# One-level Strassen passes of a GEGLU MLP: C11 kept in PSUM, staging loads issued by ScalarE, sums without negated forms

**Chip, cores, metric.** One core of one Trainium2 chip. The metric is the device time of the whole program in microseconds (us). This program runs on one core, so a single run has no state of its own; every run counted here was classed as fast.

## The reference

```python
x      (8, 1024, 1024) float32        w_gate, w_up (1024, 4096)      w_down (4096, 1024)

gate = x @ w_gate
up   = x @ w_up
gate = 0.5 * gate * (1 + np.tanh(np.sqrt(2 / np.pi) * (gate + 0.044715 * gate ** 3)))
h    = gate * up
return (h @ w_down).astype(np.float32)
```

## The kernel before

The 8192 tokens are worked off in eight passes of 1024, all in float16 with float32 sums. Passes 0 to 2 multiply gate and up with one level of a Strassen-like scheme (seven half-size products P1 to P7 in place of eight). Passes 3 to 7 use two levels with sums of weights that passes 1 and 2 have prepared and stored to HBM. After each pass comes a down product. Pass 0 loads the weights as float32 into small staging tiles and lets ScalarE cast them; passes 1 and 2 load and cast them with GpSimd. In pass 0 the kernel also forms and stores sums of w_down.

One "pair" of a one-level pass makes 256 columns of h. Its 14 slots are the products for gate (w=0) and up (w=1), each of four 512-column matmuls:

```python
SEQ = [
    ("P1", 0), ("P1", 1), ("P5", 0), ("P6", 0), ("P6", 1), ("P5", 1), ("P7", 0),
    ("P7", 1), ("P2", 0), ("P4", 0), ("P4", 1), ("P2", 1), ("P3", 0), ("P3", 1),
]
AFTER1 = {                       # work behind the product of that slot
    1: ["snap s1 0"],            # ScalarE: copy P1 out of bank "a" to SBUF ...
    2: ["snap s1 1"],
    4: ["snap s2 0"],            # ... before P6 accumulates onto the same bank
    5: ["snap s2 1"],
    7: ["snap s3 0"],
    8: ["snap s3 1", "add s3 0"],
    9: ["gelu s3", "add s3 1", "add s1 0"],
    10: ["gelu21", "prod s3", "gelu s1"],
    11: ["h21"],
    12: ["add s1 1"],
    13: ["prod s1", "add s2 0"],
    14: ["add s2 1"],
}                                # gelu s2 and prod s2 follow in the next pair
CHAIN = {"P1": "a", "P6": "a", "P7": "a", "P4": "a", "P5": "b", "P3": "b", "P2": "c"}
```

"add" is VectorE (PSUM bank plus snapshot), "gelu" ScalarE, "prod" a GpSimd product gelu(gate) x up of two SBUF tiles, "h21" a VectorE product straight from PSUM. The rest that the argument touches:

```python
def load_stage(u):               # pass 0: 512 KB of float32 weights
    ...
        nc.sync.dma_start(out=staging(u), in_=w_v[w][:, k, q * 512 : (q + 1) * 512])

def wd_store(q):                 # pass 0: seven stores of w_down sums
    ...
        nc.sync.dma_start(out=dst(v), in_=src)

def load_raw(p, q):              # passes 1 and 2: 512 columns of both weights, cast by the DMA
    ...
            nc.gpsimd.dma_start(out=raw(p, q)[:, w], in_=w_v[w][:, :, q * 512 : (q + 1) * 512])

# gate_up_one(p), pair i, q, e = divmod(i, 2)
if p == 0:
    ...
            if s // 14 == e:
                k = s % 14 + 1
                at(k, cast_stage, 8 * (q + 1) + u)       # ScalarE
                at(k, load_stage, 8 * (q + 1) + u + 4)   # into the tile just cast
    ...
elif e == 0:
    at(1, load_raw, p, q + 1)
...
if i == (12 if p == 0 else 4) and p + 1 < NPASS:
    at(2, cast_x, p + 1)         # GpSimd: the next pass's x to float16, HBM to HBM
```

## Time and profile before

| | |
|---|---|
| time, three runs | 2392.85 us median (2390.52 to 2394.59) |
| all 54 runs of this kernel in this study | 2390.2 us median and mean |
| pass 0, one-level gate and up | 252.6 us in the profile |
| passes 1 and 2, the same | 220.4 and 218.8 us |
| each two-level pass, each down product | 181.65 and 96.69 us, no gap |

In all views PE is TensorE's matmuls, PEld its weight loads, DVE VectorE, ACT ScalarE, POOL GpSimd and SP SyncE; a q behind a name is the engine's sequencer, L464 a line of the kernel, and square brackets hold the idle time before an instruction and what ended it. The page of the profiled execution gives the totals of each engine and the costliest groups (busy us, mean ns of one, idle time just before and its main releaser):

```profile
PE 2298.2 (96%) x14656; PEld 1435.1 (60%) x14656; DVE 1484.2 (62%) x2103; ACT 962.1 (40%) x1850; POOL 693.4 (29%) x821
...
L486 POOL TENSOR_TENSOR h_a<-tmp 128x512 f16<-128x512 f32 x144 | 204.9, 1424 | 447.2 <-DVE tmp L479 392.8
...
L475 ACT COPY tmp<-ps 128x512 f32<-128x512 f32 x288 | 163.7, 583 | 77.5 <-PE ps L464 74.2
```

PE is busy nearly all the time, so only its gaps in passes 0 to 2 can be won. The two groups are those that the change touches: 144 GpSimd products, a third of which (those of s1) go away, and 288 ScalarE copies, a third of which get another destination. The views of waits, chain and windows stand in the prediction.

### The profile page before, as it was taken

What the parts mean: (1) busy time and instruction counts of PE and PEld (TensorE: products, weight loads), DVE (VectorE), ACT (ScalarE), POOL (GpSimd) and SP (SyncE); (2) the same over time, 40 slices, a digit from 0 to 9 for tenths busy, and PEclk for the clock granted to TensorE, in tenths of its full rate; (3) what the DMA queues carried; (4) which work ended last, traced back from release to release, by engine and by line L of the source; (5) the groups of instructions that cost most, each with busy time, mean ns of one, the idle gap of its engine ahead of it and who ended that gap; (6) DMA issues with size and microseconds to landing.
All of it is one profiled execution on the core that took longest, in us unless ns stands there. A gap on an engine that the chain in (4) does not pass through costs nothing.

```text
span 2392.6 us, 38449 instructions
## 1 busy us (share of the span) xinstructions
PE 2298.2 (96%) x14656; PEld 1435.1 (60%) x14656; DVE 1484.2 (62%) x2103; ACT 962.1 (40%) x1850; POOL 693.4 (29%) x821
## 2 busy tenths in 40 slices
PE   6977999899999899999999999999999999999999
PEld 3433444344444344688747886488846887478854
DVE  5855627888358885467735677266754667356760
ACT  5755205454034551255403552155512554045520
POOL 1432203332023330045402542044401443024520
PEclk9988999999999999999999999999999999999999
DMA  8989757978679887798858988599867988578862
GB/s 277 281 228 251 233 153 191 214 182 236 213 172 226 190 222 248 248 307 288 269 196 268 314 279 258 195 274 324 274 219 245 310 282 273 196 269 277 281 212 106
DMA packets 259944, 579.23 MB, mean 242 GB/s; under 512 B 76016, under 2 KB 119024, under 8 KB 244976
## 3 DMA queue, kind: packets, MB, share of 16 engines
q1 hardware_dynamic: 221312, 520.16, 64.6%
q0 software_dynamic: 38448, 56.63, 14.0%
q8 instruction: 114, 1.87, 0.3%
q14 instruction: 70, 0.57, 0.1%
HBM read 520.09 MB, written 113.25 MB: 265 GB/s over the span
## 4 chain that ended last, share of the span: by engine, by line
PE 64%; DMA 5%; DVE 1%; issue 1%; POOL 0%; ACT 0%; SPq 0%; POOLq 0%; DVEq 0%; ACTq 0%
PE ps L665 38%; PE ps L760 24%; DMA ring<-in_w_up_dram 4%; PE ps L464 2%; DVE ring L294 1%; DVE tmp L479 0%; DMA w_ops<-x_sums 0%; POOL ring L279 0%; DVE x_sums L198 0%; POOL h_a L486 0%; ACT tmp L475 0%; DVE h_s L198 0%; DVE h_a L494 0%; ACT tmp L716 0%; SPq L383 0%
## 5 line engine op out<-in xcount | busy, mean ns | idle before, releaser
L665 PEld LDWEIGHTS <-ring 128*128 128x128 f16 x8320 | 812.9, 98 | 96.4
L642 POOL TENSOR_TENSOR h_a<-tmp 128x256 f16<-128x256 f32 x600 | 438.4, 746 | 954.3 <-ACT tmp L630 898.4
L760 PE MATMUL ps<-ring,h_a 128*128 128x512 f16 x3072 | 665.7, 379 | 0.0
L665 PE MATMUL ps<-x_sums,ring 128*128 128x256 f16 x5760 | 654.9, 273 | 0.0
L464 PEld LDWEIGHTS <-ring 128*128 128x128 f16 x2688 | 267.1, 99 | 422.7 <-issue 114.8
L760 PEld LDWEIGHTS <-h_a 128*128 128x128 f16 x3072 | 300.2, 98 | 361.8
L464 PE MATMUL ps<-x_sums,ring 128*128 128x512 f16 x1536 | 371.8, 393 | 76.2 <-ACT tmp L475 68.4
L627 DVE TENSOR_TENSOR tmp<-tmp,ps 128x512 f32<-128x512 f32 x600 | 387.1, 684 | 89.5 <-ACT tmp L612 63.4
L612 ACT COPY tmp<-ps 128x512 f32<-128x512 f32 x480 | 280.2, 585 | 272.4 <-PE ps L665 106.4
L716 ACT ACTIVATE tmp<-ps 128x512 f32<-128x512 f32 x128 | 76.4, 597 | 690.2 <-PE ps L760 690.2
L625 DVE TENSOR_TENSOR tmp<-ps,tmp 128x512 f32<-128x512 f32 x320 | 213.6, 688 | 214.9 <-PE ps L665 131.0
L486 POOL TENSOR_TENSOR h_a<-tmp 128x512 f16<-128x512 f32 x144 | 204.9, 1424 | 447.2 <-DVE tmp L479 392.8
L665 PE MATMUL ps<-x_b,ring 128*128 128x256 f16 x2560 | 305.6, 273 | 0.0
L630 ACT ACTIVATE tmp<-tmp 128x256 f32<-128x256 f32 x600 | 241.3, 416 | 136.4 <-DVE tmp L627 89.5
L720 DVE SCALAR_TENSOR_TENSOR tmp<-ps,tmp 128x512 f32<-128x512 f32 x96 | 66.4, 692 | 350.8 <-ACT tmp L716 218.0
L464 PE MATMUL ps<-x_b,ring 128*128 128x512 f16 x1152 | 269.4, 384 | 4.3 <-ACT ring L272 2.3
L479 DVE TENSOR_TENSOR tmp<-ps,tmp 128x512 f32<-128x512 f32 x288 | 190.1, 681 | 126.4 <-ACT tmp L475 118.6
L475 ACT COPY tmp<-ps 128x512 f32<-128x512 f32 x288 | 163.7, 583 | 77.5 <-PE ps L464 74.2
L294 DVE TENSOR_TENSOR ring<-ring 128x1024 f16<-128x1024 f16 x192 | 159.6, 845 | 22.1 <-DMA ring<-in_w_up_dram 17.9
L484 ACT ACTIVATE tmp<-tmp 128x512 f32<-128x512 f32 x144 | 90.9, 631 | 188.8 <-DVE tmp L479 188.8
L760 PE MATMUL ps<-ring,h_s 128*128 128x512 f16 x512 | 111.8, 380 | 0.0
L724 DVE TENSOR_TENSOR h_a<-h_a,h_a 128x2048 f16<-128x2048 f16 x96 | 110.3, 1216 | 0.0
(62 smaller groups left out, 691.9 us busy)
## 6 DMA issues: line engine op xcount, KB each, us to landing
ring<-w_ops SPq DMA_DIRECT2D x480, 512.0 KB, 4.5
ring<-wd_ops SPq DMA_DIRECT2D x112, 1024.0 KB, 5.0
out_dram<-tmp SPq DMA_DIRECT2D x128, 256.0 KB, 2.8
w_ops<-x_sums SPq DMA_DIRECT2D x110, 256.0 KB, 6.0
w_ops<-h_s SPq DMA_DIRECT2D x82, 256.0 KB, 5.7
ring<-in_w_gate_dram POOLq DMA_DIRECT2D x16, 1024.0 KB, 11.4
ring<-in_w_up_dram POOLq DMA_DIRECT2D x16, 1024.0 KB, 19.1
x_sums<-in_w_gate_dram SPq DMA_DIRECT2D x30, 512.0 KB, 6.0
```

The source lines that it names most:

```text
L294: nc.vector.tensor_tensor(o, a, b, op)
L464: nc.tensor.matmul(ps(b, w), lhs[:, k], rhs[:, k, :], start=(first and k == 0), stop=(k == KH - 1), skip_group_check=True,)
L475: nc.scalar.copy(tl((n, w)), ps("a", w))
L479: nc.vector.tensor_tensor(o, ps(b, w), o, ADD)
L486: nc.gpsimd.tensor_tensor(hq[TO[n]][:, i, :], tmp[:, t[n, 1]], tmp[:, t[n, 0]], MUL)
L612: nc.scalar.copy(tmp[:, t[o[1]]], ps_all[:, bank[o[2]]])
L625: nc.vector.tensor_tensor(d, b, a, SUB)
L627: nc.vector.tensor_tensor(d, a, b, ADD if o[4] == "add" else SUB)
L630: nc.scalar.activation(d, d, GELU, scale=GSC)
L642: nc.gpsimd.tensor_tensor(h, tmp[:, t[o[1]], MQ : 2 * MQ], g, MUL)
L665: nc.tensor.matmul(ps_all[:, bank[c], w * MQ : (w + 1) * MQ], lhs[:, w, k], rhs[:, k], start=(first and w == 0 and k == 0), stop=(k == KH ...
L760: nc.tensor.matmul(ps_all[:, bank[b, g]], lhs[:, j, g * P : (g + 1) * P], dc[:, n, :], start=(first and j == 0), stop=(j == NP - 1), skip_ ...
```

## The change

Its intent: C11, the quarter of the result that is P1 + P2, need not be summed by VectorE. If ScalarE copies P1 into a fresh PSUM bank, P2 can accumulate there; then gelu reads PSUM and VectorE makes the product as it does for h21. Staging loads leave SyncE's queue, where they stood behind stores. The tables of the two-level scheme are replaced by ones whose sums of weights need no negation. Cut to its core:

```diff
-    (8, 'add', 2, 3), (9, 'neg', 0, 1), ...            # A_SUMS: 3 'neg', now none
+    (8, 'add', 5, 7), (9, 'sub', 6, 0), ...
 ... (X_SUMS, A_ENTRIES, PRODUCTS, A_PARTS, AFTER likewise)
 def load_stage(u):
-            nc.sync.dma_start(
+            nc.scalar.dma_start(
 AFTER1 = {
-        1: ["snap s1 0"],
-        2: ["snap s1 1"],
+        1: ["copy 0"],
+        2: ["copy 1"],
...
-        9: ["gelu s3", "add s3 1", "add s1 0"],
-        10: ["gelu21", "prod s3", "gelu s1"],
+        9: ["gelu11", "gelu s3", "add s3 1"],
+        10: ["gelu21", "prod s3"],
         11: ["h21"],
-        12: ["add s1 1"],
-        13: ["prod s1", "add s2 0"],
+        12: ["h11"],
+        13: ["add s2 0"],
...
-            first = name in ("P1", "P5", "P2")
+            first = name in ("P1", "P5")
+            elif op == "copy":
+                w = int(n)
+                bank["c", w] = ps_free.popleft()
+                nc.scalar.copy(ps("c", w), ps("a", w))
...
-                        (0, wd_load, (n, 0)), (3, wd_load, (n, 1)),      # slots of w_down work
-                        (6, wd_load, (n, 2)), (9, wd_load, (n, 3)),
-                        (15, wd_sums, (0,)), ... (20, wd_store, (n,)),
+                        (0, wd_load, (n, 0)), (2, wd_load, (n, 1)),
+                        (4, wd_load, (n, 2)), (6, wd_load, (n, 3)),
+                        (14, wd_sums, (0,)), ... (19, wd_store, (n,)),
... (the down product gets the same copy of P1 into a PSUM bank)
+    def write_banks(banks):                              # at the start: 8 + 4 matmuls
+        for b in banks:
+            nc.tensor.matmul(
+                ps_all[:, b], identity, x0_f16[:, 0, 0:MH],
+                start=True, stop=True, skip_group_check=True,
+            )
```

> **What bounds the kernel now.** The program runs three one-level passes (0 to 2; matmul line L464), five two-level passes (3 to 7; L665) and after each a down product (L760). I first read the chain that ended last, in order of time:
>
> ```profile
> 711.11 0.93 POOL ring L279
> 712.04 19.83 DMA ring<-in_w_up_dram
> ...
> 731.97 0.69 DVE ring L294
> 732.66 0.60 DVE tmp L479
> 733.26 0.60 DVE ring L294
> 733.86 1.67 DVE h_s L198
> 735.53 0.60 DVE tmp L479
> ...
> 737.53 0.81 POOL h_a L486
> 738.34 0.66 issue
> 739.00 0.93 POOL ring L279
> ...
> 900.28 96.69 PE ps L760 x448
> 996.97 181.65 PE ps L665 x1664
> ```
>
> From 900.28 us to the end there is only PE: every down product takes 96.69 us, every two-level pass 181.65 us, without a gap. So one 512-column matmul costs 96.69/448 = 0.2158 us. A one-level pass has 896 of them: 193.4 us if PE never waits. The PE timeline puts pass 0 at 14.96 to 267.53 (252.6 us), pass 1 at 364.23 to 584.67 (220.4), pass 2 at 681.36 to 900.11 (218.8). They lose 59.2, 27.0 and 25.4 us, together 111.6; with 15 us of start, 126.6 us is all that any change outside the arithmetic can win, 5.3% of the time. A gain over 2% must remove 47.9 of it.
>
> Next, who waits, from the table of waits:
>
> ```profile
> PE ps L464 <- ACT tmp L475: 68.4, 42, 8.9
> ...
> ACT ring L259 <- DMA x_sums<-in_w_up_dram: 18.6, 6, 9.3
> ```
>
> PE waits almost only for the ScalarE copies of P1, P6 and P7 ("snaps", L475), since the next product accumulates on the copied bank. The question is what delays ScalarE. It differs by pass. Busy time by stretch (window, PE, PEld, DVE, ACT, POOL, granted clock, DMA share, GB/s):
>
> ```profile
> 54.80:153.00 98.20, 90.88 (x409) 40.16 (x408) 76.70 (x103) 65.73 (x101) 38.44 (x38) 0.98 0.95 266
> 153.00:267.50 114.50, 91.17 (x380) 38.91 (x380) 60.62 (x84) 56.91 (x89) 34.99 (x34) 0.88 0.79 223
> 364.20:584.70 220.50, 200.21 (x898) 88.34 (x897) 184.32 (x254) 113.25 (x184) 79.57 (x61) 0.98 0.82 205
> ```
>
> Pass 0 after its first pair: 409 and 380 matmuls cost 88.3 and 82.0 us, so 9.9 and 32.5 us are lost, with the DMA engines at 0.95 of their time in the first stretch. In the second, ScalarE stands in casts (L259) whose staged weights have not landed. SyncE had issued them late: at 150.8 it starts seven stores of w_down sums that take until 156.0, and only then four staging loads in a row, the first of which lands after 11 us; PE stands still for 8.9 us. In 175 to 180 the DMA engines then move almost nothing (share 0.01).
>
> Passes 1 and 2: the first fence shows a closed loop. The weight load through GpSimd takes 20 us; VectorE stands before its first weight sum until it lands, then runs sums and "adds" in order; the last add releases GpSimd's product of s2; behind that product GpSimd issues the next load. 711.11 to 739.00 is 27.9 us for two pairs, where PE needs 112 x 0.2158 = 24.2. One free interval and seven of 28.0 make 220.2, the pass as measured. The ScalarE wait is only where it shows.
>
> One step in that loop is longer than it should be:
>
> ```profile
> 733.43 1.55 POOL L486 TENSOR_TENSOR h_a<-tmp 128x512 f16<-128x512 f32 x1 [3.12 <-DVE tmp L479]
> 733.77 1.76 DVE L198 TENSOR_TENSOR h_s<-ring,x_sums 128x1024 f16<-128x1024 f16 x1
> ```
>
> This VectorE sum takes 0.68 us elsewhere. Here it overlaps GpSimd's product of s1 and ends 0.55 us after it.
>
> **What the Trainium skill says.** "SBUF — State Buffer", section "SBUF: two separate sides": VectorE with two SBUF inputs and GpSimd share a port pair as an exclusive lock, and the loser waits for the whole instruction. The two lines above agree (1.76 against 0.68). "PSUM — Partial Sum Buffer", section "The four PSUM rules": ScalarE writes neither set nor clear the bits that decide between accumulate and overwrite. That explains the added identity matmuls, which set them; the trace before cannot show it. The same page, "Specifications (TRN2)": ScalarE writes faster to PSUM than to SBUF; the trace has only copies to SBUF (583 ns), so I count no gain. "DMA: Bandwidth & Descriptors", section "Issuing engines are not separate DMA queues": another issuing engine saves only its sequencer's time, the 16 engines stay shared. The 0.95 share says that this matters in pass 0.
>
> **The change, part by part.**
>
> *C11 in PSUM, passes 0 to 2.* Per pair it removes two VectorE adds (681 ns) and one GpSimd product (1424 ns), and adds a VectorE product h11 (about 684 ns, as h21). ScalarE keeps its count: two copies and a gelu. VectorE thus saves 0.68 us per pair, 33 us over 48 pairs, GpSimd 68 us; neither is a bound as a total. What counts is the loop. Between landing and GpSimd's s2 product VectorE still runs seven instructions, since h11 takes the place of the second add. But the s1 product, the collision partner, is gone: 1.67 becomes 0.60. The loop goes from 27.9 to 26.8 us, still above 24.2. Seven intervals times 1.07 us in two passes: -15 us; I take 14.
>
> *PSUM banks.* Six of eight are held by a pair, as before; the copies take theirs at slots 1 and 2 instead of 9 and 12. By first-in-first-out order each bank needed was freed at least four slots earlier. No new wait.
>
> *Sums without negated forms.* 48 half-size instructions (L200, 46.9 us together) become 24 whole ones of 0.68 to 0.9 us, about 20 us: 27 us less VectorE work in passes 1 and 2, but mostly early in a pair, off the loop. Worth nothing by itself while the loop is the bound. X_SUMS gain two negated forms per pass, about +1 us each in the down product, where VectorE is 42% busy (40.92 of 96.70): free.
>
> *Staging loads on ScalarE's queue, w_down loads earlier.* Loads no longer sit behind stores that wait for sums; w_down data get one or two slots (0.9 to 1.7 us) more. Nearly all of the 32.5 us should open up. But each load now occupies ScalarE, behind its own cast: 0.37 us (the duration of the same issue on SyncE). In slots 3 to 20 of each block of 28, ScalarE has 8 casts x 1.05, 9 snaps x 0.58 and 4 gelus x 0.63 = 16.1 us for 17 x 0.863 = 14.7 us; with 8 issues, 19.1. Snaps have about two slots of slack; walking through the block I get some 2.3 us of PE waiting, 16 us over seven blocks. DMA work after the first pair is 0.95 x 98.2 + 0.79 x 114.5 = 184 us, so it cannot be short either. 789 x 0.2158 = 170 + 16 + 10 for loads landing late = 196 instead of 212.7: -16.5 us.
>
> *Start.* Twelve identity matmuls. Eight follow the first transposes, while PE waits anyway; four must wait for ScalarE's evictions (end 31.0), and P5's first product, now at 26.25 in an idle hole, goes behind them: +2.5 us with the slow clock there.
>
> *Two-level passes.* Same 208 matmuls per block. By count: 13 snaps for 12, 24 accumulations as before, 16 gelus and GpSimd products for 15 plus one from PSUM. ScalarE 13 x 0.585 + 16 x 0.416 = 14.3 of 22.7 us, VectorE 24 x 0.686 = 16.5, GpSimd 16 x 0.746 = 11.9. In both tables the shortest distance from a reader of a chain to its next product is two slots, from freeing a bank to its use seven before and six after, tiles at least seven: 0 us. The down product: the same snaps plus 32 copies, minus 32 adds; each copy has three groups, 5.2 us: 0 us.
>
> Sum: 2392.85 + 2.5 - 14 - 16.5 = 2364.9, say 2365 us (-1.2%).
>
> **Rivals.** *ScalarE becomes the bound in pass 0*: its total is against it (65.73 of 98.20 busy), the dense half of the block for it. If an issue costs 0.6 us rather than 0.37, pass 0 gains nothing: 2381. *DMA is the bound in pass 0 whatever issues*: 0.95 speaks for it, 0.01 at 175 against; 2375. *The loop opens*: if loads take 18 us because stores spread better, or less VectorE work lets GpSimd issue early, passes 1 and 2 reach about 200 us each: 2340. For it: VectorE loses over 1.5 us per pair. Against: the two loads (1024 KB each as float16, so 4.2 MB of float32 read) already share the engines with the stores of the sums, at a 0.82 DMA share. *A two-slot distance in the new table is missed*: 40 blocks make each 0.5 us into 20 us, 2385 or more; the distance occurs before too, without any gap.
>
> **Range and chances.** Good luck in both pass 0 and the loop gives 2340, an overloaded ScalarE 2388. Over 2% needs under 2345, that is the loop opening as well as pass 0: 0.14. Slower needs a broken two-level pass: 0.02.
>
> **What would show it.** L665 still 181.65 us per pass and L760 96.69; passes 1 and 2 near 212 us with GpSimd issues 26.8 us apart and the sum before the s2 add at 0.68; pass 0 near 238 us, casts waiting little for DMA, snaps delayed by the issues instead. I am wrong if passes 1 and 2 fall near 200, if the ScalarE issue is much cheaper or dearer than 0.37 us, or if L665 has gaps.

## The result

Ratios here are the mean time of one kernel's fast runs over the mean of the other's fast runs of the same rounds, so they are not quite the ratios of the medians quoted beside them.

The changed kernel took **2379.88 us** median (2376.07 to 2380.98, three runs) against 2392.85: ratio 0.9943 [0.9920, 0.9965]. A later set of six gave 2379.3 us (2372.44 to 2384.78), ratio 0.9961. The nine together have a median of 2379.88 us and a mean of 2379.0, 11.2 us under the mean of the kernel before. The result is correct.

The page after, the same parts:

```profile
PE 2296.5 (97%) x14668; PEld 1436.8 (61%) x14668; DVE 1357.1 (57%) x1959; ACT 1013.9 (43%) x1922; POOL 662.5 (28%) x813
...
L488 POOL TENSOR_TENSOR h_a<-tmp 128x512 f16<-128x512 f32 x96 | 147.9, 1541 | 504.1 <-ACT tmp L486 369.2
```

VectorE lost 127 us of work and GpSimd 48 products, as intended. The kernel won a tenth of that. Windows of pass 0 from 55 us on and of pass 1 (window, busy time of PE, PEld, DVE, ACT, POOL, granted clock, DMA share, GB/s):

```profile
55.00:262.80 207.80, 183.40 (x807) 79.98 (x806) 121.64 (x175) 127.02 (x195) 56.36 (x58) 0.97 0.89 252
359.60:573.40 213.80, 199.33 (x897) 88.56 (x896) 149.29 (x222) 112.26 (x184) 62.24 (x45) 0.98 0.85 212
```

In pass 1 VectorE went from 184.32 to 149.29 us of work, and the pass from 220.4 to 213.9. The chain that ended last shows why no more (start, us, engine, tile, line):

```profile
493.28 0.69 DVE ring L295
493.98 0.60 DVE h_a L499
495.69 0.68 DVE tmp L481
496.98 0.61 DVE tmp L481
498.26 0.99 issue
499.25 0.93 POOL ring L280
500.18 19.84 DMA ring<-in_w_up_dram
520.11 0.69 DVE ring L295
...
978.53 181.65 PE ps L668 x1664
```

It is the loop of before, with a shorter way through VectorE: weights land, VectorE runs in order to the last add of s2 (496.98), GpSimd issues the next load (499.25), 20 us pass. The period is 26.83 us here (493.28 to 520.11), still above the 24.2 that PE needs. The two-level passes are unchanged at 181.65 us. The table of waits (total us, times, longest):

```profile
PE ps L462 <- DVE tmp L481: 20.9, 11, 2.4
PE ps L462 <- ACT tmp L473: 19.0, 13, 5.9
...
PE ps L462 <- ACT ps L478: 7.5, 8, 2.1
...
ACT tmp L473 <- DMA wd_ops<-h_s: 5.0, 1, 5.0
```

PE's wait for ScalarE's copies fell from 68.4 us to 19.0 + 7.5, but 20.9 us now show as a wait for VectorE's adds, of which the table before has none: 19.8 of them lie in passes 1 and 2, where the loop still sets the pace. The last line is new: a ScalarE copy from PSUM is held by a *store* of w_down sums, with which it has nothing to do. Pass 0 took 247.2 us. Where it stands still is best seen in the timeline around 80 us:

```profile
73.35 0.37 ACTq L253 DMA_DIRECT2D x_sums<-in_w_gate_dram  x1
...
73.77 1.04 ACT L260 CAST ring<-x_sums 128x1024 f16<-128x1024 f32 x1 [0.45 <-ACT ring L260]
...
78.28 1.05 ACT L260 CAST ring<-x_sums 128x1024 f16<-128x1024 f32 x1
...
83.84 0.37 ACTq L253 DMA_DIRECT2D x_sums<-in_w_up_dram  x1
84.31 1.07 ACT L473 COPY tmp<-ps 128x512 f32<-128x512 f32 x2 [4.98 <-DMA wd_ops<-h_s]
84.95 3.57 PE L462 MATMUL ps<-x_sums,ring 128*128 128x512 f16 x8 [4.64 <-ACT tmp L473]
```

and around 228 us:

```profile
227.42 1.04 ACT L260 CAST ring<-x_sums 128x1024 f16<-128x1024 f32 x1 [6.25 <-DMA x_sums<-in_w_up_dram]
...
229.00 3.57 PE L462 MATMUL ps<-x_sums,ring 128*128 128x512 f16 x8 [5.88 <-ACT tmp L473]
```

The kernel before had its two longest standstills of pass 0 here:

```profile
168.73 1.87 PE L464 MATMUL ps<-x_sums,ring 128*128 128x512 f16 x4 [8.90 <-ACT tmp L475]
...
230.75 3.57 PE L464 MATMUL ps<-x_sums,ring 128*128 128x512 f16 x8 [7.00 <-ACT tmp L475]
```

The fences of after show three different things. At 73 us ScalarE issues a staging load into the tile that it has just cast: it waits for its own cast to be done, issues for 0.37 us, and starts the next cast 0.45 us late. At 83.84 us an issue comes 4.5 us after its cast has ended, and PE stands still for 4.64 us. At 227 us a cast waits for weights that have not landed, and PE stands still for 5.88 us; the kernel before has this gap too (7.00 us), the one at 84 us it has not.

**How far one profile can be trusted.** A stage's time differs between executions. The kernel before and two of the variants below run the very same instructions in pass 0 (b_early, b_tab); their pass 0 ended at 267.5, 261.8 and 261.4 us, 263.6 on average. Four profiles of the changed pass 0 (after twice, a_early, a_early_prod) ended at 262.9, 264.1, 263.5 and 263.5, 263.5 on average. So the 5 us that pass 0 seems to have won in the first two profiles are not borne out: **on these averages it won nothing.** Passes 1 and 2 took 219.2 us each on average in four profiles with the old loop (before, b_act, b_castx, b_act_late; 217.4 to 221.0), 214.5 in seven with the new one (after twice, a_sp, a_oldwd, a_late, a_castx, a_wdpool; 211.5 to 220.4): 9.4 us for both. That accounts for most of the 11.2. The sets of runs were made on different chips; the medians of the kernel before in the five later sets lie between 2389.5 and 2391.7 us, so medians of different sets compare to about 2 us.

### The profile page after: what moved, and what is told of

The parts are those of the page before. It is cut to its first block, busy times and chain, and to the rows that moved or that the text cites. A ratio compares the mean times of both kernels' runs of the same rounds, so it can differ in the third digit from the quotient of the medians.

```text
span 2374.2 us, 38264 instructions
## 1 busy us (share of the span) xinstructions
PE 2296.5 (97%) x14668; PEld 1436.8 (61%) x14668; DVE 1357.1 (57%) x1959; ACT 1013.9 (43%) x1922; POOL 662.5 (28%) x813
## 4 chain that ended last, share of the span: by engine, by line
PE 79%; DMA 13%; DVE 3%; ACT 2%; issue 1%; POOL 1%; SPq 0%; ACTq 0%; POOLq 0%; DVEq 0%
PE ps L668 38%; PE ps L763 33%; DMA ring<-in_w_up_dram 9%; PE ps L462 8%; DVE ring L295 1%; DMA h_s<-in_w_down_dram 1%; DMA wd_ops<-h_s 1%; DVE tmp L481 1%; ACT ring L260 1%; DMA x_sums<-in_w_up_dram 1%; DVE h_a L499 1%; DMA h_a<-in_w_gate_dram 1%; DMA h_a<-in_w_up_dram 0%; POOL h_a L488 0%; POOL ring L280 0%
## 5 line engine op out<-in xcount | busy, mean ns | idle before, releaser
L645 POOL TENSOR_TENSOR h_a<-tmp 128x256 f16<-128x256 f32 x640 | 464.6, 745 | 928.2 <-ACT tmp L633 893.4
L630 DVE TENSOR_TENSOR tmp<-tmp,ps 128x512 f32<-128x512 f32 x640 | 413.8, 683 | 220.1 <-PE ps L668 166.5
L462 PE MATMUL ps<-x_sums,ring 128*128 128x512 f16 x1536 | 366.2, 388 | 47.5 <-DVE tmp L481 20.9
L615 ACT COPY tmp<-ps 128x512 f32<-128x512 f32 x520 | 304.3, 585 | 203.5 <-PE ps L668 127.0
L633 ACT ACTIVATE tmp<-tmp 128x256 f32<-128x256 f32 x640 | 263.8, 418 | 173.0 <-DVE tmp L628 80.3
L488 POOL TENSOR_TENSOR h_a<-tmp 128x512 f16<-128x512 f32 x96 | 147.9, 1541 | 504.1 <-ACT tmp L486 369.2
L628 DVE TENSOR_TENSOR tmp<-ps,tmp 128x512 f32<-128x512 f32 x240 | 165.4, 689 | 151.6 <-ACT tmp L615 104.2
L723 DVE SCALAR_TENSOR_TENSOR tmp<-ps,tmp 128x512 f32<-128x512 f32 x64 | 44.2, 691 | 302.6 <-ACT tmp L719 248.4
L481 DVE TENSOR_TENSOR tmp<-ps,tmp 128x512 f32<-128x512 f32 x192 | 129.6, 684 | 152.2 <-ACT tmp L473 150.6
L295 DVE TENSOR_TENSOR ring<-ring 128x1024 f16<-128x1024 f16 x192 | 137.3, 728 | 39.2 <-DMA ring<-in_w_up_dram 35.0
L473 ACT COPY tmp<-ps 128x512 f32<-128x512 f32 x192 | 111.5, 585 | 90.4 <-PE ps L462 77.6
L486 ACT ACTIVATE tmp<-tmp 128x512 f32<-128x512 f32 x96 | 60.2, 627 | 164.8 <-DVE tmp L481 163.0
```

Of the source, the lines that this page charges most:

```text
L295: nc.vector.tensor_tensor(o, a, b, op)
L462: nc.tensor.matmul(ps(b, w), lhs[:, k], rhs[:, k, :], start=(first and k == 0), stop=(k == KH - 1), skip_group_check=True,)
L473: nc.scalar.copy(tl((n, w)), ps("a", w))
L481: nc.vector.tensor_tensor(o, ps("b", w), o, ADD)
L488: nc.gpsimd.tensor_tensor(hq[TO[n]][:, i, :], tmp[:, t[n, 1]], tmp[:, t[n, 0]], MUL)
L615: nc.scalar.copy(tmp[:, t[o[1]]], ps_all[:, bank[o[2]]])
```

## The experiments

"Before" and "after" are the two kernels. Each label starts with the one that it is built on. The theory after the first look: the closed loop hides the worth of C11 in passes 1 and 2; in pass 0 the ScalarE queue trades one kind of wait for another, while the cast of x at 227 us stays. Rivals: the new tables rather than C11 shortened the loop; DMA bandwidth alone limits pass 0; the w_down slots do harm; ScalarE is the bound in passes 1 and 2.

### The parts one by one

**a_sp**: after, with `nc.scalar.dma_start(out=staging(u)` back on `nc.sync`.

> The changed kernel with only the staging loads put back on SyncE's queue. In the changed kernel the loop of passes 1 and 2 gave 13.8 us (pass 1 220.4 to 213.9, pass 2 218.8 to 211.5) and pass 0 only 5.4 (252.6 to 247.2), where I had forecast 14 net. Theory S: the ScalarE queue gives little, because each issue holds ScalarE for about 0.5 us behind its own cast and some issues wait for stores; then this kernel is within 5 us of the changed one, pass 0 between 243 and 252 us. Rival Q: the queue gives what I forecast (16 us) and the start took it back; then pass 0 here is 258 us or more and the kernel 11 us or more slower than the changed one. Passes 1 and 2 unchanged at 214 and 212 in both.

2384.1 us (2379.92 to 2384.69), ratio 0.9971 [0.9959, 0.9984]. Pass 0 ended at 267.3 us, passes 1 and 2 took 215.6 and 213.9. So the queue is worth about 4 us on the changed kernel, in pass 0; against the spread of after (2372 to 2385) that is not much, and a_sp_ec below measures it better (there with the late issue).

**b_act**: the reverse, before with only the staging loads on ScalarE.

> The kernel before with only the staging loads moved to ScalarE's queue. Theory S: pass 0 within 6 us of 252.6, on either side, passes 1 and 2 as before (220, 219), total 2387 to 2398. Rival Q: pass 0 at 240 or less, total 2381 or less.

2393.72 us (2392.41 to 2396.07), ratio 1.0018 [1.0005, 1.0030]: alone, this part makes the kernel slightly *slower*. PE's standstill of 8.9 us at 168 us is gone, but there are new ones of 2.5 and 4.4 us; ScalarE stood 7.0 us for w_down stores.

**b_psum**: before with only C11 in PSUM (pair, down product, identity matmuls), old tables, queue and slots.

> The kernel before with only C11 summed in PSUM (and the identity matmuls that this needs). If removing the s1 product from GpSimd is what shortened the loop, passes 1 and 2 fall here by most of the 13.8 us, to about 214 to 215 and 212 to 213, and the sum that took 1.76 us in the loop takes 0.68. If instead the sums without negated forms did it, they stay near 220 and 219. Pass 0 loses 3 to 5 us at the start in both; total 2382 to 2388 in the first case, 2396 in the second.

2384.36 us (2381.58 to 2387.95), ratio 0.9978 [0.9965, 0.9992]; passes 1 and 2 at 214.7 and 217.2 us, 3.2 us less than with the old loop on average, where the whole change has 4.7 (pass 2 was expected at 212 to 213). So C11 shortens the loop without the new tables, by about two thirds of what the whole change does; this is one profile.

**b_tab**: before with only the new tables.

> The kernel before with only the new tables (sums without negated forms, and the product order that belongs to them). If the sums matter only by VectorE's load, which is not in the loop, passes 1 and 2 stay within 2 us of 220 and 219 and the whole within 5 us of the kernel before; if VectorE's load is what bounds those passes, they fall by 5 us or more each. Two-level passes 181.65 us in either case.

2387.07 us (2382.6 to 2389.65), ratio 0.9985 [0.9970, 1.0000]; 217.1 and 219.3 us. About 27 us less VectorE work in these passes, and nothing or almost nothing won: it lay off the loop. The rival falls.

**a_oldwd**: after with the old slots of the w_down work (0, 3, 6, 9; 15 to 18; 20).

> The changed kernel with the old slots of the w_down loads, sums and stores. Both theories: within 4 us of the changed kernel (2376 to 2384), since VectorE waits for those loads only 16 us in all and the largest wait, 11.9 us near 219 to 231, is a load behind the cast of the next x, which this does not move.

2387.39 us (2384.05 to 2388.02), ratio 0.9987 [0.9974, 0.9999]. With the old slots ScalarE stood for w_down stores three times, for 4.8, 3.3 and 2.4 us, and PE's standstill at the cast of x grew to 8.63 us. The earlier slots are worth some 8 us, almost twice what I had expected at most; they do no harm.

### Is it the load loop that limits passes 1 and 2?

**a_early**: after, with each GpSimd load issued one slot earlier, ahead of the product of s2 in GpSimd's order. The ring buffer that it fills is free by then.

```diff
-            elif e == 0:
-                at(1, load_raw, p, q + 1)
+            elif i == 0:
+                at(1, load_raw, p, 1)
+            elif e == 1:
+                at(14, load_raw, p, q + 2)
```

> The changed kernel, with the weight load of passes 0-free 1 and 2 issued on GpSimd after product 14 of the odd pair, ahead of that pair's s2 product, instead of behind it. Theory L (the loop load, sums, adds, s2 product, next load bounds passes 1 and 2): the adds and the s2 product leave the loop; what stays is load 20 us, issue 0.93, and sum, h11, sum, entry of about 2.6: 23.5 us, under PE's 24.2. Passes 1 and 2 then take 194 to 199 us each instead of 214 and 212, the whole 2345 to 2353. Rival D (the DMA engines, at 0.85 of their time there, are the bound): the loads stretch with the earlier issue and the passes stay above 207.

2346.56 us (2345.02 to 2348.33), ratio 0.9815 [0.9800, 0.9830]: 33 us less than after, all of it in passes 1 and 2, now 199.8 and 197.2 us. The window of pass 1:

```profile
360.20:560.00 199.80, 194.26 (x897) 87.50 (x896) 152.86 (x222) 111.73 (x184) 60.92 (x45) 1.00 0.91 227
```

VectorE and ScalarE run as many instructions as in after (222 and 184) in 14 us less (152.86 against 149.29 and 111.73 against 112.26 us busy), and PE is near its 193.4. So neither of them was the bound, and the loop was.

**b_early**: the same edit on before. What is the change worth once the loop is open?

> The kernel before with the early weight load. If the same loop bounds it, with its longer step only inside the loop: passes 1 and 2 fall from 220 and 219 to 196 to 203, the whole to 2348 to 2360. Since VectorE is busy 184 of 220 us there, it may become the bound instead: then 204 to 210 each, and the difference to the changed kernel's 200 and 197 is what C11 and the sums are worth by themselves.

2374.09 us (2371.43 to 2374.67), ratio 0.9930 [0.9918, 0.9941]; 209.9 and 212.1 us. With the loop open the change is worth 27.5 us (2374.09 to 2346.56); with it closed, 11 to 13. What holds b_early is in its timeline:

```profile
383.26 1.55 POOL L486 TENSOR_TENSOR h_a<-tmp 128x512 f16<-128x512 f32 x1 [1.58 <-DVE tmp L479]
383.61 1.75 DVE L198 TENSOR_TENSOR x_sums<-h_s 128x1024 f16<-128x1024 f16 x1
...
385.28 0.68 DVE L479 TENSOR_TENSOR tmp<-ps,tmp 128x512 f32<-128x512 f32 x1
...
387.15 1.02 PE L464 MATMUL ps<-x_sums,ring 128*128 128x512 f16 x4 [0.88 <-ACT tmp L475]
```

GpSimd's product of s1 (383.26) stretches a VectorE sum to 1.75 us; the add of s2 follows right behind it at 385.28, ScalarE's gelu and copies behind that add, and PE waits 0.88 us. Such gaps of 0.88 and 1.04 us come in every pair, every 13.1 to 13.3 us.

**a_early_prod**: a_early, with one GpSimd product per pair put back in passes 1 and 2, in the place of the old product of s1. Its result is wrong on purpose: it overwrites a quarter of h. VectorE and ScalarE keep the instructions of a_early. The product's two input tiles come free later than in a_early (the edit leaves this out); no instruction waits for them in its trace.

```diff
-        13: ["add s2 0"],
+        13: ["again", "add s2 0"],
...
+            elif op == "again":
+                if p > 0:
+                    nc.gpsimd.tensor_tensor(
+                        hq["a11"][:, i, :], tmp[:, t["s3", 1]], tmp[:, t["s3", 0]], MUL
+                    )
+                    tmp_free.extend((t["s3", 0], t["s3", 1]))
```

> The changed kernel with the earlier weight loads, and in passes 1 and 2 one GpSimd product per pair put back where the removed product of s1 stood (wrong result on purpose: it overwrites a quarter of h). VectorE and ScalarE have the same instructions as in the kernel with the earlier loads alone. Theory: with the load loop open, it is this GpSimd product, which holds up a VectorE sum (1.75 us) just ahead of the adds of s2, that made the regular gaps of 0.9 to 1.0 us per pair in the kernel before with earlier loads; then the gaps come back at each pair, passes 1 and 2 take 208 to 213 us and the kernel 2368 to 2374 us. Rival: VectorE's two adds fewer (and its shorter weight sums) made the difference; then the passes stay at 197 to 202 us and the kernel at 2345 to 2352. In between, both have a part.

2364.42 us (2363.27 to 2365.36), ratio 0.9898 [0.9884, 0.9913]; 208.2 and 205.9 us. The gaps came back, smaller in all than expected (2368 to 2374 us), because mostly in every second pair (PE timeline of this kernel):

```profile
388.04 4.48 PE L462 MATMUL ps<-x_sums,ring 128*128 128x512 f16 x20 [0.89 <-DVE tmp L481]
413.30 4.48 PE L462 MATMUL ps<-x_sums,ring 128*128 128x512 f16 x20 [0.93 <-DVE tmp L481]
```

The chain of this kernel leads through the stretched sum (at 384.56 us, 1.67 us; 0.60 at the same place in a_early) and the adds of s2 into the gap at 388.04. The product alone costs 17.9 us of the 27.5 (2364.42 against 2346.56). It is the larger part; the rest, some 10 us, goes with everything else that differs (two VectorE adds fewer and one product more per pair, the shorter weight sums, the copies into PSUM), which no run separates further.

### Pass 0: what replaced the waits for loads

**a_late**: after, each staging load issued one slot after its cast, `at(k + 1, load_stage, ...)` for `at(k, ...)`. The intent: ScalarE no longer waits for the cast just started.

> The changed kernel with each staging load issued one product later than its cast, so that ScalarE's queue need not wait for the cast to end. Theory S (ScalarE's issue behind its own cast costs 0.45 us of ScalarE each, and that delays its copies): the 0.45 us waits behind casts vanish and pass 0 falls from 247 to 233 to 240 us, the whole 7 to 14 us faster than the changed kernel. Rival D0 (pass 0 is bound by the DMA engines, at 0.89): pass 0 stays within 4 us of 247 or grows, because the loads start 0.86 us later.

2369.88 us (2366.47 to 2376.93), ratio 0.9919 [0.9902, 0.9936]; pass 0 ended at 253.4 us instead of 263.5. A group of 20 matmuls across the end of the second pair (its last 12 and the first 8 of the third), from which I measure below, starts at 54.8 us, in four profiles of after at 58.1 to 60.0. Only about half of the waits went, though: in pass 0 ScalarE waited 28 times for its own cast in after, 12.6 us in all, and still 13 times, 5.8 us, in a_late. The edit also shifts each load and its place among the copies, so that these waits make the whole 10 us is not shown.

**b_act_late**: the same on b_act.

> The kernel before with the staging loads on ScalarE's queue, each issued one product after its cast. With the issue directly behind the cast it took 2393.7 (pass 0 252.0). Theory S: without the 0.45 us waits pass 0 is 240 to 246 and the whole 2380 to 2387. If waits for stores are the reason, pass 0 stays at 249 to 253.

2385.92 us (2382.51 to 2387.18), ratio 0.9982 [0.9970, 0.9994], against 2393.72 without: 7.8 us. The issue directly behind its own cast was costly whatever else was changed. One slot later the ScalarE queue alone does pay, by 4 us.

**a_wdpool**: after with the w_down stores issued by GpSimd (`nc.gpsimd.dma_start(out=dst(v), in_=src)`). This tests why a staging load on ScalarE waits for a w_down store. In the program as compiled (it is a matter of the program, not of the chip) the DMAs of SyncE and ScalarE take their completion semaphores in turn from one set of eight, and a DMA waits for the earlier one on its semaphore. GpSimd's DMAs are not in that set.

> The changed kernel with the stores of the w_down sums issued by GpSimd instead of SyncE. In the compiled program the DMAs of SyncE and ScalarE take their completion semaphores in turn from one set of eight, so that a staging load on ScalarE waits for the store that had its semaphore before; in the changed kernel ScalarE stood 7.5 us for such stores. In this program no staging load waits for a store. Theory M (shared semaphores): ScalarE's waits for stores go to 0, the 4.6 us standstill of PE near 81 us goes, pass 0 falls by 5 to 9 us to 238 to 242. Rival: the stores' traffic itself holds the loads up; then the wait turns into one for the staged weights and pass 0 stays within 3 us of 247.

2385.21 us (2384.7 to 2388.52), ratio 0.9976 [0.9963, 0.9988]: slower than after. PE's timeline:

```profile
80.06 1.89 PE L462 MATMUL ps<-x_sums,ring 128*128 128x512 f16 x8 [0.22 <-ACT tmp L473]
...
236.84 1.87 PE L462 MATMUL ps<-x_sums,ring 128*128 128x512 f16 x4 [10.70 <-ACT tmp L473]
```

The mechanism is shown. In the packed trace of after (the instructions' operands, which no view prints) the DMAs of SyncE and ScalarE name the same eight semaphores and those of GpSimd eight others, and the load issued at 83.84 us waits for the one that a store issued at 76.48 us completes at 83.76. In a_wdpool ScalarE no longer waits for any w_down store, and the 4.64 us are 0.22. The gain that I had put to it did not come: around the cast of x a ScalarE cast now waits 11.4 us for its weights (4.64 us were won, 4.8 more lost there than in after), and pass 0 ended at 269.7 us. That GpSimd, with the stores in its queue, starts the w_down loads and the cast of x at a worse moment is my reading; no run separates it.

**a_castx**: after, with the cast of the next x at pair 14 instead of 12 of pass 0.

> The changed kernel with the cast of the next x in pass 0 issued two pairs later, after the last staging loads. If the 5.9 us standstill of PE near 223 us (and the slow clock after it, some 1.7 us) is a staging load that shares the DMA engines with this cast and four w_down loads, it goes and the kernel gains 5 to 8 us. If the w_down loads alone make it, under 2 us.

2370.35 us (2368.0 to 2374.14), ratio 0.9918 [0.9904, 0.9931]. Pass 0 ended at 256.6 us, with no standstill near 228 us. The gain is a little more than the 5 to 8 us expected.

**b_castx**: the same on before.

> The kernel before with the cast of x two pairs later. It has the same standstill (7.0 us near 226 us). If the cast of x makes it in this kernel too: 5 to 9 us faster than the kernel before, pass 0 at 244 to 248. If it is SyncE's queue behind the stores: within 2 us.

2381.19 us (2378.13 to 2383.9), ratio 0.9962 [0.9951, 0.9974], 9 us under before. So this loss is independent of the queue. The cast of x is one 2 MB write with its reads; that it slows the staging loads by sharing their DMA engines fits, but only the time of the cast was varied. The other standstills of before stay in this run (4.24, 7.20, 4.16 us); those were the ones that a queue move could touch.

**after_again**: the changed kernel unchanged, because its time rested on three runs.

> The changed kernel once more, because its time rests on three runs and the single parts of pass 0 are worth 6 to 10 us each. If the three runs stand for it, it comes out at 0.993 to 0.996 of the kernel before, 2375 to 2381 us. If the three runs were lucky, at 0.996 or more, and the issue beside its own cast, the w_down slots and the queue were then worth less than stated; if they were unlucky, at 0.992 or less.

2379.3 us (2372.44 to 2384.78), ratio 0.9961 [0.9945, 0.9977]. The median stands; by the ratio, which falls just on the side where I had called the first three runs lucky (0.996 or more), the gain is 0.4 to 0.6%. In its profile pass 2 took 220.4 us, with loads of 22.4, 23.3 and 22.7 us on the chain: in the closed loop a slow load goes straight into the time.

### Together

**a_elc**: after with the three edits early load, late issue and later cast of x.

> The changed kernel with all three repairs: early weight load, staging issue one product later, cast of x two pairs later. If their gains add (33.3, 10.0 and 9.5 us by the medians), 2327; the late issue and the later cast both work on pass 0, so rather 2327 to 2335, pass 0 at 230 to 236, passes 1 and 2 at 196 to 200.

2331.22 us (2329.43 to 2335.75), ratio 0.9751 [0.9737, 0.9764]: the fastest of the study, 2.5% under before. Pass 0 ended at 245.8 us; passes 1 and 2 took 200.1 and 197.3. The wait for a w_down store is still in it (ScalarE 4.8 us, PE 4.06 us at 82 us), since a_wdpool's way out costs more than it gives.

**a_sp_ec**: the staging loads on SyncE again, early load and later cast of x.

> The changed kernel with the staging loads on SyncE, early weight load and later cast of x: what ScalarE's queue is worth once the other waits are gone. If the queue with the later issue is worth what the late issue alone gave over SyncE (2384 against 2370), this is 12 to 18 us slower than the version on ScalarE's queue, about 2343 to 2350, pass 0 at 244 to 250; if SyncE's waits came mostly from the cast of x, it is within 5 us of it.

2342.13 us (2340.75 to 2344.85), ratio 0.9795 [0.9781, 0.9808]. Next to a_elc on the same chip, ScalarE's queue with the late issue is worth 10.9 us (12 to 18 expected).

**a_elcw**: a_elc with the w_down stores on GpSimd.

> The same, with the stores on GpSimd too. Theory M: another 4 to 8 us, 2320 to 2329, pass 0 at 224 to 230. Rival as for the stores alone: no faster than without it.

2342.52 us (2338.68 to 2344.8), ratio 0.9794 [0.9781, 0.9807]: 11 us slower than a_elc. I had expected 4 to 8 us gained. Here too the stores are better left on SyncE, shared semaphores or not.

**a_start**: a_elc with fewer identity matmuls at the start: two instead of eight, and one instead of four, issued later (`write_banks((ps_free[1], ps_free[3]))`, and the last bank's at slot 13).

> The version with the three repairs, with three identity matmuls instead of twelve: two before the first product, for the two banks that its copies use, and one after product 13 of the first pair, for the only transposed bank that is copied into next. If the identity matmuls make the start's cost, P5's first product is back in the hole before 31 us, the second pair's last four products begin 2 to 3 us earlier (near 55 instead of 58 us), and the whole is 2 to 3 us faster than 2331. If ScalarE's copies and casts make it, under 1 us.

2331.73 us (2329.15 to 2334.37), ratio 0.9756 [0.9743, 0.9769]: no difference. The same group of 20 matmuls started 2.0 us earlier (54.2 against 56.2 us), but pass 0 ended no earlier (248.0 against 245.8). The profiled run of a_start was its slowest (2334.37 us), so one pair of profiles can't settle why pass 0 gave the 2 us back.

## Why the prediction was right or wrong

**The bound and its proof hold.** The two-level passes and down products stayed at 181.65 and 96.69 us with the new tables. All the difference lies in the one-level passes.

**Start, +2.5: right.** In kernels with C11 in PSUM and SyncE's queue (a_sp, b_psum, a_sp_ec), that group of 20 matmuls starts at 55.9, 53.9 and 54.8 us, against 52.6 on average in before, b_early, b_tab and b_castx: +2.2. The four identity matmuls do wait for ScalarE's evictions (PE timeline of after):

```profile
32.23 2.05 PE L829 MATMUL ps<-h_a,identity 128*128 128x512 f16 x4 [7.55 <-ACT x_b L228]
```

**Loop, -14: right in mechanism, too large.** The VectorE sum in the loop fell from 1.67 to about 0.60 us, as written, and b_psum shows that C11 did it. The passes won 4.7 us each, not 7. The term that failed is "Seven intervals times 1.07 us": I held the load at 20 us and took all intervals as equal, and they are not. GpSimd's load issues in passes 1 and 2 are 26.4 to 30.9 us apart in four profiles with the old loop, 28.4 on average, and 25.9 to 31.0 in two of after, 27.9 on average: 0.5 us less each, not 1.07. The slower of the two loads of a step lands 19.2 us after its issue with the old loop and 20.2 in after (means of the passes' medians), so the faster loop gave part of its gain back in longer loads. That the loads, stores and sums now crowd the DMA engines more (share 0.82 before, 0.85 after in pass 1) is my reading, not shown.

**Pass 0, -16.5: this step failed.** In the prediction's words: "Loads no longer sit behind stores that wait for sums ... Nearly all of the 32.5 us should open up", less 16 us for the overloaded ScalarE and 10 for late loads. I compare the time that PE loses from that group of 20 matmuls to the end of pass 0, where 796 matmuls need 796 x 0.2158 = 171.8 us.

| us | forecast | measured |
|---|---|---|
| lost before the change | 42.4 | 42.7 in the profile that I read; 39.2 on average with b_early and b_tab |
| lost after it | 26 | 32.5 on average of four profiles |
| lost earlier, in the first block, by the queue move | 0 | 4.4 (start at 59.2 instead of 54.8 us) |
| gain | 16.5 | 39.2 - 32.5 - 4.4 = 2.3, lost in the spread |

So 3.2 us of the forecast were an unlucky profile, 6.5 us were losses that I had not counted or had thought open, and 4.4 us came ahead of the stretch that I had worked out. Behind the last two stand three causes:

- *The issue behind its own cast* was foreseen, but only for the seven later blocks; the first block has the same and loses the 4.4 us. a_late wins 10.1 us of pass 0, 4.4 of them in the first block and 5.7 after it, where the prediction had 16 us of cost; as about half of the waits remain in a_late, how much 16 was too large is not settled. Over the whole of pass 0 it decides whether the queue move is a gain or a loss (b_act against b_act_late).
- *A new wait, not in the sum.* An issue on ScalarE waits for a store of SyncE. The Trainium skill, "DMA: Bandwidth & Descriptors", section "Anatomy of one DMA — SWDGE (gpsimd) path", says that any semaphore wait of a DMA happens on the issuing sequencer before dispatch. I had read of the sequencer time saved and not drawn this conclusion. The trace agrees: ScalarE idle for 4.98 us and PE for 4.64 at 84 us. In the kernel before, such a wait could only stop SyncE.
- *The standstill at the cast of x, put to the wrong cause.* It was part of the 32.5 us, and I let the queue move open it. It stayed at 5.88 us; a later cast of x removed it, at 9 us of the total in both kernels.

PE's standstills of over 1.5 us in this stretch add up to 25.7 us in before's profile and 14.3 in after's, 10.5 of which are the last two causes. The move did open the standstills of 8.9 and 4.1 us at 168 and 196 us, as forecast: with SyncE's queue, a_sp has 6.17 and 4.67 us there.

**The rivals.** "The loop opens" was the right thing to watch: it did not open by itself, but one issue moved by a slot opens it and gives 33 us. My price for it, 200 us a pass, is what a_early shows. "ScalarE becomes the bound in pass 0" was right in part: not by its total, but by what stands in its queue. "DMA is the bound whatever issues" falls: a_elc moves the same bytes and ends pass 0 18 us earlier than after.

**What remains open**: what gives back a_start's 2 us, which of the other differences carries the last 10 us of b_early against a_early, and how much of the late issue's 10 us is the wait for the own cast.

## What to carry to other kernels

Before you credit work removed from an engine, find the loop that sets the pace and ask what stays in it: here 35 us less VectorE work per pass gave 5, and a load issued one slot earlier gave 16 more, after which one removed GpSimd product per pair was alone worth 18 us over two passes. When a DMA issue moves to a compute engine, everything that the issue waits for (its buffer, the last cast from it, the completion it shares with other transfers) becomes a wait of that engine, so place it where these are long past. Compare stages over several profiles: the first two showed a gain of 5 us in pass 0 that five more did not.

## What the Trainium skill lacked or had wrong

- "DMA: Bandwidth & Descriptors", section "Issuing engines are not separate DMA queues": it names only the sequencer time that is saved. It lacks the cost on the other side (that the wait happens on the issuer is said elsewhere on the page, without a price): a load moved to ScalarE took 0.37 us to issue and delayed the next cast by 0.45 us behind its own cast, and one load held ScalarE 4.98 us for a store issued by SyncE. Alone, the move made the kernel 0.18% slower.
- No page has it that two issuing engines can share completion semaphores through the program as compiled (eight for SyncE and ScalarE here), so that a transfer of one waits for a transfer of the other (a_wdpool: 4.64 us of PE's wait became 0.22 when the stores moved to GpSimd).
- "PSUM — Partial Sum Buffer", section "Specifications (TRN2)": ScalarE faster to PSUM than to SBUF holds, but no size is given; a 128x512 float32 copy took 567 ns to PSUM and 585 ns to SBUF.
